# Eight shared PSUM banks divided into four and four, and VectorE's element-wise operations in the form with three operands

## The chip, the core and the metric

The kernel runs on one core of a Trainium2 chip, in one launch. The metric is the device time of the execution in microseconds (us), read on the chip. The engines are TensorE (PE; PEld is its loading of weights), VectorE (DVE), ScalarE (ACT) and GpSimd (POOL); SyncE (SP) issues most of the DMAs. PSUM, in which TensorE leaves its products, has eight banks of 512 float32 values on each of 128 partitions.

## What is computed

Two blocks of two layers each, on one sequence of 1024 tokens with 1024 channels, all in float32:

```python
def reference(x, ...):
    x = first_block(x, ...)
    return second_block(x, ...)

# first_block, twice:
h = rms_norm(x, norm_w[layer])
q, k, v, z_attn, q_h, f_h, i_h, g_h, gate_attn, gate_hgrn = split(h @ w_in[layer])
a = sliding_window_attention(rope(q), rope(k), v, sinks) * silu(z_attn)
b = rms_norm(hgrn2_recurrence(silu(q_h), k_of(f_h), i_h, logf)) * w * silu(g_h)
merged = sigmoid(gate_attn) * (a @ w_up_attn[layer]) + sigmoid(gate_hgrn) * (b @ w_up_hgrn[layer])
x = x + merged @ w_out[layer]
# and a last rms_norm

# second_block, layer 0:
u, v, z = split(rms_norm(x, g) @ w_in)
x = x + (gelu(u) * (W_s @ layer_norm(gelu(v)) + b) * silu(z)) @ w_out
# layer 1: k and v of the stream; each chunk of 64 tokens attends to itself and 8 chunks before
x = x + (chunk_attention(q, k, v, bias) * silu(z)) @ w_out
# and a last rms_norm
```

The sliding-window attention has 8 query heads and 2 key heads of 64 channels and a window of 128; the chunk attention has 16 heads of 64.

## The kernel before

Activations lie transposed (channels on partitions, 512 tokens to a tile) in tiles of 128x512 float32 from one heap of 61 (`hp`). For accuracy every operand of a large product is split in a rounded part and a rest, `hi` and `lo` (for weights `wh` and `wl`): `lo = x - hi` is an element-wise subtraction, and each product is three matmuls. Weights come from HBM through `raw` tiles (three buffers) and are split into eight `wh` and eight `wl` tiles.

The Python program is a list of units. A unit loads and splits its weights, two units ahead of its use, takes a PSUM tile with `mm()`, sets its matmuls (`unit`, L261 to L263, 512 columns or, in the last part, 256; `unit_tok`, L275 to L277, 256 columns; `unit_wide`, L289 to L291), and gives the result to a small function that evicts it. All other work is written as generators ("fibers"), which advance a step for every 24 matmuls or so (in the chunk attention 8). What they put in PSUM goes into tiles of `aux()`: means of squares over the channels (L383, L1027 and, for the first quarter and the second of the tokens, L1163), transposed keys (L573) and queries, scores of the sliding window (L634), levels of the recurrence (L703), a bias of the gMLP layer (L1234, L1239) and the chunk attention's scores (L1424), transposed probabilities (L1460) and output (L1470). `mm()` and `aux()` take their tiles from one ring of eight:

```python
    def mm(self):
        return self.ps.tile([P, H], F32, tag="bank", bufs=8, name=self.name("mm"))
    def aux(self):
        return self.ps.tile([P, H], F32, tag="bank", bufs=8, name=self.name("aux"))
```

So the tile that is ninth in the program waits until the first has been read, whichever of the two it is. Engines work on their own queues; the order of instructions on each queue is set ahead of the run by a list scheduler, which takes the program's order, the dependencies and its own estimates of time, and may set a later matmul ahead of an earlier one whose operand it expects later. It doesn't set an instruction ahead if that needs a buffer which is still in use.

Element-wise work is given to VectorE, GpSimd or ScalarE by a running account of booked time (`Engine.load`, `least`). All calls of an engine pass one helper, so that in the profile nearly all rows but TensorE's have its line, L76; tiles tell them apart. `khl` is a split key of one block of 128 tokens (two buffers), `ropea` and `ropeb` are parts of the rotation, `sP` the probabilities and `pT` their transposed form.

In the chunk attention the work goes by blocks of one pair of heads and 128 queries, 64 in all: two or four score tiles, a softmax, up to four tiles of transpositions, one output tile `po`, which ScalarE copies out. At the very end `out_last` (L1000) makes the output in quarters of 256 tokens: product, residual, sum of squares, mean (L1027), scaling, store.

Of the kernel before, what the change touches and what calls it, by code (L numbers as in the profile page):

```python
# [9 lines left out]
F32 = mybir.dt.float32  # L10
# [4 lines left out]
ALU = mybir.AluOpType  # L15
# [4 lines left out]
P = 128  # L20
H = 512
# [60 lines left out]
class Chip:  # L82
# [5 lines left out]
    def least(self, names, method, n):  # L88

        return min((getattr(self, k) for k in names), key=lambda e: e.load + e.price(method, n))  # L90

    def spend(self, ns):
        for e in (self.vector, self.scalar, self.gpsimd):
            e.load = max(0.0, e.load - ns)


class Net:
# [44 lines left out]
        return self.heap(F32R), self.heap(F32R)  # L142

    def mm(self):
        return self.ps.tile([P, H], F32, tag="bank", bufs=8, name=self.name("mm"))

    def aux(self):
        return self.ps.tile([P, H], F32, tag="bank", bufs=8, name=self.name("aux"))

    def half_banks(self):  # L150

# [47 lines left out]
    def tt(self, out, in0, in1, op):  # L199

        e = self.nc.least(("vector", "gpsimd"), "tensor_tensor", int(np.prod(out.shape[1:])))
        e.tensor_tensor(out=out, in0=in0, in1=in1, op=op)

    def split(self, src, hi, lo, hsrc=None):
        self.copy(hi, src)
# [191 lines left out]
    def square_sum(self, acc, x, k, scale=None):  # L397
        nc = self.nc
        if k == 0:
            acc = self.heap()  # L400
            sq = acc
        else:
            sq = self.heap()
        if scale is None:
            nc.scalar.activation(out=sq, in_=x, func=AF.Square)
        else:
            nc.scalar.activation(out=sq, in_=x, func=AF.Square, scale=scale)
        if k:
            nc.vector.tensor_add(acc, acc, sq)
        return acc  # L410

    @contextmanager
# [587 lines left out]
    def out_last(self, ws, wload, rhs, xsrc, gain):  # L1000

        nc = self.nc
        Q = 256
        xs = {}
        pair = lambda t, k, qs: t[2 * k : 2 * k + 2, 1, :, qs].rearrange("k p t -> p k t")

        def run(q, j):
            qs = slice(q * Q, (q + 1) * Q)
            if q == 0 and j < KD - AHEAD:
                wload(j + AHEAD)  # L1010
            if j % 2 == 0:
                xs[j // 2] = self.heap().rearrange("p (k t) -> p k t", k=2)
                nc.sync.dma_start(out=xs[j // 2], in_=pair(xsrc, j // 2, qs))
            ps = self.mm()[:, :Q]
            self.unit(ps, ws[j], [[None, tuple(t[:, qs] for t in r[1])] for r in rhs], 1)
            x = xs[j // 2][:, j % 2, :]
            nc.vector.tensor_add(x, ps, x)
            sq = self.heap()[:, :Q]
            nc.scalar.activation(out=sq, in_=x, func=AF.Square)
            if j == 0:  # L1020
                xs["acc"] = sq
            elif j < KD - 1:
                nc.vector.tensor_add(xs["acc"], xs["acc"], sq)
            else:
                po = self.aux()[:, :Q]
                for i, t in enumerate((xs["acc"], sq)):
                    nc.tensor.matmul(po, self.ones_f, t, start=(i == 0), stop=(i == 1))  # L1027
            nc.scalar.activation(out=x, in_=x, func=AF.Copy, scale=gain(j))
            if j == KD - 1:
                r = self.rstd_of(po, Q)  # L1030
                for k in range(KD // 2):
                    x = xs[k]
                    (nc.gpsimd if k == 1 else nc.vector).tensor_tensor(
                        out=x, in0=x, in1=r[:, None, :].to_broadcast([P, 2, Q]), op=ALU.mult
                    )
                    (nc.nc.scalar if k % 2 and q else nc.sync).dma_start(out=pair(self.out, k, qs), in_=x)
            self.tick(1.5 * len(rhs))

        for q in range(2):
            for j in range(KD):  # L1040
                self.units.append((None, lambda w, q=q, j=j: run(q, j)))
# [18 lines left out]
    def scaled_split(self, xs, ks, gain, rstd, res, half):  # L1060
        nc = self.nc
        for k in ks:
            t = xs[k]
            if gain is None:
                nc.vector.tensor_mul(t, t, rstd[half])
            else:
                nc.vector.scalar_tensor_tensor(
                    out=t, in0=t, scalar=gain(k), in1=rstd[half], op0=ALU.mult, op1=ALU.mult
                )
            res[k][half] = self.split_pair(t)  # L1070
        yield
# [67 lines left out]
    def load_first(self, res):  # L1139

        nc = self.nc
        Q = 256
        xs = [self.heaps(KD // 2) for _ in range(2)]
# [8 lines left out]
        def squares(q):  # L1152
            acc = None
            for x in xs[q]:
                sq = self.heap()
                nc.scalar.activation(out=sq, in_=x, func=AF.Square)
                if acc is None:
                    acc = sq
                else:
                    nc.vector.tensor_add(acc, acc, sq)  # L1160
            ps = self.aux()[:, :Q]
            for i in range(2):
                nc.tensor.matmul(ps, self.ones_f, acc[:, i * Q : (i + 1) * Q], start=(i == 0), stop=(i == 1))  # L1163
            return ps

        def scale(q, r):
            o = slice(q * Q, (q + 1) * Q)
            for k in range(KD):
                x = xs[q][k // 2][:, (k % 2) * Q : (k % 2) * Q + Q]
                nc.vector.scalar_tensor_tensor(  # L1170
                    out=x, in0=x, scalar=self.col("norm_w", k), in1=r, op0=ALU.mult, op1=ALU.mult
                )
                if q == 0:
                    res[k][0] = self.pair()
                hi, lo = res[k][0]
                nc.scalar.copy(out=hi[:, o], in_=x)
                e = nc.gpsimd if k % 2 else nc.vector
                e.tensor_tensor(out=lo[:, o], in0=x, in1=hi[:, o].bitcast(F32), op=ALU.subtract)

        r = self.rstd_of(squares(0), Q)  # L1180
        root = self.root
# [62 lines left out]
    def gmlp_half(self, h, half, y, ready):  # L1244
        nc, a = self.nc, self.a
# [42 lines left out]
        def mix(hd, z, u, wm, bias):  # L1288
            yield
            self.finish(st["ln"])  # L1290
            pm = self.aux()
            s = slice((hd % 4) * P, (hd % 4) * P + P)
            for t in range(4):
                nc.tensor.matmul(pm[:, t * P : (t + 1) * P], v[t][hd // 4][:, s], wm[:, s], start=True, stop=True)
            m = self.heap()
            nc.vector.scalar_tensor_tensor(
                out=m.rearrange("p (g t) -> p g t", g=4), in0=pm.rearrange("p (g t) -> p g t", g=4),
                scalar=self.col("a_ln_g", hd), in1=bias[:, None, s].to_broadcast([P, 4, P]),
                op0=ALU.mult, op1=ALU.add,
            )  # L1300
            yield
            nc.vector.tensor_mul(m, m, u)
            self.tt(m, m, z, ALU.mult)
            y[hd][half] = self.split_pair(m)

# [409 lines left out]
```

## Time and profile before

| | us |
|---|---|
| median of three runs (3022.23 to 3022.83) | 3022.28 |
| the profiled execution | 3024.32 |
| its span, from the first instruction to the last | 3022.5 |
| TensorE busy | 2927.0 |
| VectorE busy | 1678.1 |
| ScalarE busy | 1449.5 |
| GpSimd busy | 1091.5 |

Busy time counts the time in which an engine executes; the chain that ended last goes over TensorE for 89% of the span and over VectorE for 4%. The mean granted clock of TensorE over the span is 0.99 of its full speed (2.4 GHz); the profile has it in shares of that.

### The profile page before, as it was taken

What the parts mean: (1) busy time and instruction counts of PE and PEld (TensorE: products, weight loads), DVE (VectorE), ACT (ScalarE), POOL (GpSimd) and SP (SyncE); (2) the same over time, 40 slices, a digit from 0 to 9 for tenths busy, and PEclk for the clock granted to TensorE, in tenths of its full rate; (3) what the DMA queues carried; (4) which work ended last, traced back from release to release, by engine and by line L of the source; (5) the groups of instructions that cost most, each with busy time, mean ns of one, the idle gap of its engine ahead of it and who ended that gap; (6) DMA issues with size and microseconds to landing.
All of it is one profiled execution on the core that took longest, in us unless ns stands there. A gap on an engine that the chain in (4) does not pass through costs nothing.

```text
span 3022.5 us, 43638 instructions
## 1 busy us (share of the span) xinstructions
PE 2927.0 (97%) x16188; PEld 2432.3 (80%) x16188; DVE 1678.1 (56%) x3298; ACT 1449.5 (48%) x2927; POOL 1091.5 (36%) x1174
## 2 busy tenths in 40 slices
PE   6999999999999999999999999999999799999997
PEld 5887887888878888788888878888888688878777
DVE  6556745556556666665666533445344644454566
ACT  4665325642357434475334455334544545564552
POOL 4445333543435433444332233213332322232331
PEclk9999999999999999999999999999999899999999
DMA  3212242122522224212243222533234111111123
GB/s 113 84 63 93 89 147 82 66 70 91 182 70 71 73 84 151 99 70 70 74 151 132 101 92 97 166 103 129 95 116 159 56 38 60 38 59 44 64 98 112
DMA packets 101493, 283.47 MB, mean 94 GB/s; under 512 B 11288, under 2 KB 15512, under 8 KB 101280
## 3 DMA queue, kind: packets, MB, share of 16 engines
q1 hardware_dynamic: 100016, 279.51, 27.3%
q8 instruction: 128, 2.10, 0.3%
q10 hardware_dynamic: 1264, 1.17, 0.1%
q14 instruction: 85, 0.70, 0.1%
HBM read 259.66 MB, written 20.97 MB: 93 GB/s over the span
## 4 chain that ended last, share of the span: by engine, by line
PE 89%; DVE 4%; issue 2%; POOL 2%; DMA 1%; ACT 1%; SPq 0%; DVEq 0%; POOLq 0%; ACTq 0%
PE mm L261 20%; PE mm L262 20%; PE mm L263 20%; PE mm L289 3%; PE mm L290 3%; PE mm L291 3%; DVE hp L76 3%; PE aux L703 2%; PE aux L1470 2%; PE aux L1424 2%; PE mm L275 2%; PE aux L1460 2%; PE mm L276 1%; PE mm L277 1%; PE aux L634 1%
## 5 line engine op out<-in xcount | busy, mean ns | idle before, releaser
L261 PE MATMUL mm<-hp,wh 128*128 128x512 f32 (+1 forms) x2816 | 1118.8, 397 | 0.0
L262 PE MATMUL mm<-hp,wh 128*128 128x512 f32 (+1 forms) x2816 | 1093.2, 388 | 2.0 <-POOL hp L76 2.0
L263 PE MATMUL mm<-hp,wl 128*128 128x512 f32 (+1 forms) x2816 | 1093.7, 388 | 0.0
L76 POOL TENSOR_TENSOR wl<-raw,wh 128x512 fp32r<-128x512 f32 x369 | 491.3, 1334 | 800.7 <-ACT wh L76 690.7
L76 ACT CAST wh<-raw 128x512 fp32r<-128x512 f32 x584 | 360.4, 620 | 692.5 <-PE mm L262 467.1
L76 POOL TENSOR_TENSOR hp<-hp,hp 128x256 f32<-128x256 f32 (+3 forms) x347 | 380.5, 1102 | 680.1 <-DVE hp L76 240.3
L261 PEld LDWEIGHTS mm<-hp,wh 128*128 128x128 f32 x2816 | 530.7, 188 | 114.9 <-issue 11.2
L263 PEld LDWEIGHTS mm<-hp,wl 128*128 128x128 f32 x2816 | 530.0, 188 | 110.9 <-issue 0.2
L262 PEld LDWEIGHTS mm<-hp,wh 128*128 128x128 f32 x2816 | 531.1, 189 | 102.0 <-POOL hp L76 3.3
L76 DVE TENSOR_TENSOR wl<-raw,wh 128x512 fp32r<-128x512 f32 x447 | 358.8, 805 | 231.8 <-ACT wh L76 188.7
L76 DVE TENSOR_TENSOR hp<-hp,hp 128x512 f32<-128x512 f32 (+2 forms) x407 | 296.3, 737 | 154.9 <-ACT hp L76 109.3
L76 ACT ACT_TABLE_LOAD x244 | 313.1, 1283 | 22.9 <-PE mm L263 10.5
L76 DVE TENSOR_TENSOR hp<-mm,hp 128x512 f32<-128x512 f32 (+2 forms) x264 | 166.6, 637 | 161.1 <-ACT hp L76 79.3
L76 ACT ACTIVATE hp<-mm 128x512 f32<-128x512 f32 (+2 forms) x304 | 171.4, 574 | 170.0 <-PE mm L291 78.8
L76 DVE CAST wh<-raw 128x512 fp32r<-128x512 f32 x232 | 118.9, 513 | 186.9 <-PE mm L262 148.9
L76 ACT CAST hp<-hp 128x512 fp32r<-128x512 f32 (+1 forms) x206 | 116.0, 574 | 217.9 <-POOL hp L76 179.8
L76 POOL TENSOR_SCALAR sP<-sP,a2l 128x640 f32<-128x640 f32 (+4 forms) x128 | 89.0, 697 | 284.4 <-DVE a2l L76 176.7
L289 PE MATMUL mm<-wh,hp 128*128 128x512 f32 x480 | 188.1, 392 | 0.0
L290 PE MATMUL mm<-wl,hp 128*128 128x512 f32 x480 | 188.1, 392 | 0.0
L291 PE MATMUL mm<-wh,hp 128*128 128x512 f32 x480 | 187.8, 391 | 0.0
L76 ACT ACTIVATE sP<-sP,a2nm 128x640 f32<-128x640 f32 (+4 forms) x128 | 88.3, 691 | 101.1 <-DVE a2nm L76 101.0
L275 PE MATMUL mm<-wh,hp 128*128 128x256 f32 x448 | 133.7, 298 | 0.0
(186 smaller groups left out, 3406.0 us busy)
## 6 DMA issues: line engine op xcount, KB each, us to landing
raw<-in_w_ch_dram SPq DMA_DIRECT2D x128, 512.0 KB, 3.3
raw<-in_g_uz_dram SPq DMA_DIRECT2D x64, 512.0 KB, 3.3
hp<-xd SPq DMA_DIRECT2D x88, 256.0 KB, 4.2
raw<-in_w_up_dram SPq DMA_DIRECT2D x64, 256.0 KB, 2.7
raw<-in_w_o_dram SPq DMA_DIRECT2D x32, 512.0 KB, 3.3
raw<-in_g_v_dram SPq DMA_DIRECT2D x32, 512.0 KB, 4.0
raw<-in_g_o_dram SPq DMA_DIRECT2D x32, 512.0 KB, 3.8
raw<-in_w_wide_dram SPq DMA_DIRECT2D x28, 512.0 KB, 3.9
```

Source lines behind the costliest of these rows:

```text
L76: self.last = f(*args, **kw)
L261: nc.tensor.matmul(ps, wh[:, c : c + P], rh, start=(k == 0), stop=False)
L262: nc.tensor.matmul(ps, wh[:, c : c + P], rl, start=False, stop=False)
L263: nc.tensor.matmul(ps, wl[:, c : c + P], rh, start=False, stop=(k == nk - 1))
L275: nc.tensor.matmul(ps, lh[:, o : o + P], wh[:, c : c + n], start=(k == 0), stop=False)
L289: nc.tensor.matmul(ps, lh[:, s], wh, start=(k == 0), stop=False)
L290: nc.tensor.matmul(ps, lh[:, s], wl, start=False, stop=False)
L291: nc.tensor.matmul(ps, ll[:, s], wh, start=False, stop=(k == KD - 1))
L703: nc.tensor.matmul(ps[:, s], k[:, s], q[:, s], start=True, stop=True)
L1424: nc.tensor.matmul(ps[:, 0:w], lhs[r, o : o + P], rhs[r, k0 : k0 + w], start=(j == 0), stop=(j == 2))
L1460: nc.tensor.transpose(ps[:, j * P : (j + 1) * P], S[:, (i + j) * P : (i + j + 1) * P], self.ident)
L1470: nc.tensor.matmul(po[e * 64 : e * 64 + 64, 0:P], vv, pts[e][:, i * P : (i + 1) * P], start=(i == 0), stop=(i == nb - 1),)
```

## The change

The ring of eight banks becomes two of four, one for the units' products and one for everything else. And where VectorE combines two tensors in SBUF by a sum, a difference or a product, the instruction is `scalar_tensor_tensor`, `(in0 * 1.0) op in1`, in place of `tensor_tensor`, `in0 op in1`; operations that read PSUM keep their form, and GpSimd's too. The new helper is `Chip.ew`.

```diff
+    def ew(self, out, in0, in1, op):
+        self.vector.scalar_tensor_tensor(out=out, in0=in0, scalar=1.0, in1=in1, op0=ALU.mult, op1=op)
...
     def mm(self):
-        return self.ps.tile([P, H], F32, tag="bank", bufs=8, name=self.name("mm"))
+        return self.ps.tile([P, H], F32, tag="mm", bufs=4, name=self.name("mm"))
     def aux(self):
-        return self.ps.tile([P, H], F32, tag="bank", bufs=8, name=self.name("aux"))
+        return self.ps.tile([P, H], F32, tag="aux", bufs=4, name=self.name("aux"))
...
         e = self.nc.least(("vector", "gpsimd"), "tensor_tensor", int(np.prod(out.shape[1:])))
-        e.tensor_tensor(out=out, in0=in0, in1=in1, op=op)
+        if e is self.nc.vector:
+            self.nc.ew(out, in0, in1, op)
+        else:
+            e.tensor_tensor(out=out, in0=in0, in1=in1, op=op)
...
         if k:
-            nc.vector.tensor_add(acc, acc, sq)
+            nc.ew(acc, acc, sq, ALU.add)
...
-                e = nc.gpsimd if k % 2 else nc.vector
-                e.tensor_tensor(out=lo[:, o], in0=x, in1=hi[:, o].bitcast(F32), op=ALU.subtract)
+                sub = nc.gpsimd.tensor_tensor if k % 2 else nc.ew
+                sub(out=lo[:, o], in0=x, in1=hi[:, o].bitcast(F32), op=ALU.subtract)
```

The same replacement stands in the sums of squares of `out_last` and `load_first`, in `scaled_split` and in the gMLP layer's product with `u`. Lines behind the helper move by a few numbers: L1163 becomes L1170, L573 L580, L634 L641, L1424 L1431.

The order of instructions changes on all queues. Three places follow. In the first a name has the number of its allocation only, in the others the tile's own number as well.

The first is the start, on TensorE. Before, the mean of the second quarter (`aux_209`) stands second, ahead of every unit:

```order
L1163 MATMUL aux_132<-hp_121,ones_f 128x256 x2
L1163 MATMUL aux_209<-hp_198,ones_f 128x256 x2
L275 MATMUL mm_299<-wh_142,hp_159 128x256
L276 MATMUL mm_299<-wl_143,hp_159 128x256
L277 MATMUL mm_299<-wh_142,hp_160 128x256
L275 MATMUL mm_299<-wh_142,hp_164 128x256
```

Now all matmuls of the two units `mm_299` and `mm_332` (24 each, with the hi and lo parts of the first quarter) and one of `mm_359` stand ahead of it; these are the rows around it:

```order
L283 MATMUL mm_332<-wl_155,hp_189 128x256
L284 MATMUL mm_332<-wh_154,hp_190 128x256
L282 MATMUL mm_332<-wh_154,hp_194 128x256
L283 MATMUL mm_332<-wl_155,hp_194 128x256
L284 MATMUL mm_332<-wh_154,hp_195 128x256
L282 MATMUL mm_359<-wh_221,hp_159 128x256
L1170 MATMUL aux_209<-hp_198,ones_f 128x256 x2
L283 MATMUL mm_359<-wl_222,hp_159 128x256
L284 MATMUL mm_359<-wh_221,hp_160 128x256
L282 MATMUL mm_359<-wh_221,hp_164 128x256
```

So the mean of the second quarter has moved 49 rows back.

The second is the first block of the chunk attention, on TensorE: `aux4253` and `aux4254` are its first scores, of the queries `hp4243` and `hp4244`. `mm4242` is the product that gives the first keys, `mm4260` one of values. Before:

```order
L262 MATMUL mm4242_20524<-hp4152_20027,wh4208_20413 128x512
L263 MATMUL mm4242_20524<-hp4151_20026,wl4209_20414 128x512
L1424 MATMUL aux4253_20567<-hp4243_20549,hp4240_20520 128x256
L1424 MATMUL aux4254_20568<-hp4243_20549,hp4240_20520 128x256
L275 MATMUL mm4260_20597<-wh4211_20421,hp4105_19829 128x256
L1424 MATMUL aux4253_20567<-hp4244_20550,hp4240_20520 128x256
L1424 MATMUL aux4254_20568<-hp4244_20550,hp4240_20520 128x256
L1424 MATMUL aux4253_20567<-hp4243_20549,hp4241_20521 128x256
L1424 MATMUL aux4254_20568<-hp4243_20549,hp4241_20521 128x256
L276 MATMUL mm4260_20597<-wl4212_20422,hp4105_19829 128x256
L277 MATMUL mm4260_20597<-wh4211_20421,hp4106_19830 128x256
```

Now these rows stand around the first scores:

```order
L282 MATMUL mm4262_20624<-wh4218_20441,hp4151_20026 128x256
L283 MATMUL mm4262_20624<-wl4219_20442,hp4151_20026 128x256
L284 MATMUL mm4262_20624<-wh4218_20441,hp4152_20027 128x256
L282 MATMUL mm4273_20676<-wh4211_20421,hp4105_19829 128x256
L1431 MATMUL aux4253_20567<-hp4243_20549,hp4240_20520 128x256
L1431 MATMUL aux4254_20568<-hp4243_20549,hp4240_20520 128x256
L1431 MATMUL aux4253_20567<-hp4244_20550,hp4240_20520 128x256
L1431 MATMUL aux4254_20568<-hp4244_20550,hp4240_20520 128x256
L1431 MATMUL aux4253_20567<-hp4243_20549,hp4241_20521 128x256
L1431 MATMUL aux4254_20568<-hp4243_20549,hp4241_20521 128x256
```

All 24 matmuls of `mm4260`, all 24 of `mm4262` and one of `mm4273` have moved ahead of the scores.

The third is the beginning of the second half of the tokens in the first block's second layer, at 1228 us, on GpSimd. `hp2363` holds two blocks of keys, `khl2383` and `khl2399`, `khl2400` split ones; `hp2395` and `hp2396` are queries. Before:

```order
L76 TENSOR_TENSOR wl2340_11194<-raw2336_11187,wh2339_11193 128x512
L76 TENSOR_TENSOR hp2363_11263<-ropea2386_11402,ropeb2387_11403 128x2x16
L76 TENSOR_TENSOR ropea2401_11506<-hp2395_11468,cos_493 128x64
L76 TENSOR_TENSOR ropeb2402_11507<-hp2395_11468,sin_494 128x4x8 x2
L76 TENSOR_TENSOR hp2395_11468<-ropea2401_11506,ropeb2402_11507 128x4x16
L76 TENSOR_TENSOR ropea2412_11604<-hp2396_11470,cos_493 128x64
L76 TENSOR_TENSOR ropeb2413_11605<-hp2396_11470,sin_494 128x4x8 x2
L76 TENSOR_TENSOR hp2396_11470<-ropea2412_11604,ropeb2413_11605 128x4x16
L76 TENSOR_TENSOR hp2405_11536<-hp2395_11468,hp2405_11536 128x4x64
L76 TENSOR_TENSOR khl2399_11496<-hp2363_11263,khl2399_11496 128x128 x2
L76 TENSOR_TENSOR khl2400_11501<-hp2363_11263,khl2400_11501 128x128 x2
```

Now:

```order
L76 TENSOR_TENSOR khl2382_11386<-hp2363_11263,khl2382_11386 128x128 x2
L76 TENSOR_TENSOR khl2383_11391<-hp2363_11263,khl2383_11391 128x128 x2
L76 TENSOR_TENSOR wl2340_11194<-raw2336_11187,wh2339_11193 128x512
L76 TENSOR_TENSOR khl2399_11496<-hp2363_11263,khl2399_11496 128x128 x2
L76 TENSOR_TENSOR khl2400_11501<-hp2363_11263,khl2400_11501 128x128 x2
L76 TENSOR_TENSOR ropea2401_11506<-hp2395_11468,cos_493 128x64
L76 TENSOR_TENSOR ropeb2402_11507<-hp2395_11468,sin_494 128x4x8 x2
L76 TENSOR_TENSOR hp2395_11468<-ropea2401_11506,ropeb2402_11507 128x4x16
L76 TENSOR_TENSOR ropea2412_11604<-hp2396_11470,cos_493 128x64
L76 TENSOR_TENSOR ropeb2413_11605<-hp2396_11470,sin_494 128x4x8 x2
L76 TENSOR_TENSOR hp2396_11470<-ropea2412_11604,ropeb2413_11605 128x4x16
L76 TENSOR_TENSOR hp2405_11536<-hp2395_11468,hp2405_11536 128x4x64
```

The subtractions of `khl2399` and `khl2400` have moved ahead of the rotation of the queries; on ScalarE their casts have moved in the same way ahead of the eviction of the queries.

## Rows read from the trace of the kernel before

**Rows 1.** The page, busy time of each engine, its share and instructions.

```profile
PE 2927.0 (97%) x16188; PEld 2432.3 (80%) x16188; DVE 1678.1 (56%) x3298; ACT 1449.5 (48%) x2927; POOL 1091.5 (36%) x1174
```

**Rows 2.** TensorE in order of time, 7 to 45 us: start, length, instructions [idle before].

```profile
27.15 2.08 PE L1163 MATMUL aux<-hp,ones_f 128*128 128x256 f32 x4 [17.40 <-DVE hp L76]
```

**Rows 3.** TensorE in order of time, 2344 to 2371 us.

```profile
2343.70 0.39 PE L262 MATMUL mm<-hp,wh 128*128 128x512 f32 x1
...
2346.64 0.39 PE L263 MATMUL mm<-hp,wl 128*128 128x512 f32 x1
2363.40 0.58 PE L1424 MATMUL aux<-hp,hp 64*128 64x256 f32 x2 [16.37 <-ACT hp L76]
...
2367.63 0.28 PE L275 MATMUL mm<-wh,hp 128*128 128x256 f32 x1
...
2370.98 0.28 PE L276 MATMUL mm<-wl,hp 128*128 128x256 f32 x1
```

**Rows 4.** Waits of TensorE: line, releaser: total us, times, longest.

```profile
PE aux L573 <- POOL khl L76: 7.6, 5, 3.0
PE aux L634 <- ACT hp L76: 4.4, 11, 0.9
...
PE aux L1239 <- ACT hp L76: 3.1, 4, 1.1
```

**Rows 5.** Stretches: busy us of PE, PEld, DVE, ACT, POOL (instructions), clock, DMA share, GB/s.

```profile
1207.00:1210.40 3.40, 3.40 (x19) 3.40 (x18) 1.28 (x1) 2.35 (x4) 3.09 (x11) 0.51 0.00 0
...
1230.90:1237.80 6.90, 6.51 (x20) 5.16 (x21) 2.65 (x7) 2.17 (x9) 1.58 (x4) 0.51 0.10 38
1691.70:1695.10 3.40, 3.40 (x10) 2.68 (x9) 2.94 (x8) 1.90 (x3) 0.00 (x0) 0.50 0.57 200
...
2372.00:2875.00 503.00, 502.08 (x3586) 411.69 (x3586) 244.09 (x860) 265.21 (x686) 141.40 (x186) 1.00 0.15 53
...
2985.40:2988.80 3.40, 3.40 (x16) 3.22 (x15) 2.71 (x4) 1.19 (x3) 0.00 (x0) 0.50 0.80 298
```

**Rows 6.** TensorE in order of time, 1201 to 1234 us.

```profile
1205.79 0.50 PE L383 MATMUL aux<-hp,ones_d 128*128 128x512 f32 x1 [3.48 <-DVE hp L76]
...
1227.98 0.28 PE L573 MATMUL aux<-identr,khl 128*128 128x128 f32 x1 [2.20 <-ACT khl L76]
1231.29 0.91 PE L573 MATMUL aux<-identr,khl 128*128 128x128 f32 x4 [3.03 <-POOL khl L76]
```

**Rows 7.** TensorE in order of time, 2978 to 2990 us.

```profile
2984.81 0.70 PE L1027 MATMUL aux<-hp,ones_f 128*128 128x256 f32 x2 [2.58 <-DVE hp L76]
```

**Rows 8.** VectorE's groups by form: busy us, mean ns, idle us before them.

```profile
L76 DVE TENSOR_TENSOR wl<-raw,wh 128x512 fp32r<-128x512 f32 x447 | 358.8, 805 | 231.8 <-ACT wh L76 188.7 <-PE aux L383 14.8 <-PE aux L784 12.8
...
L76 DVE TENSOR_TENSOR hp<-hp,hp 128x512 f32<-128x512 f32 x139 | 119.1, 872 | 39.6 <-ACT hp L76 27.6 <-DMA hp<-xd 8.8
...
L76 DVE SCALAR_TENSOR_TENSOR hp<-hp,hp 128x512 f32<-128x512 f32 x52 | 45.9, 883 | 0.5
```

**Rows 9.** Waits of TensorE from 59 to 72 us.

```profile
PE aux L573 <- POOL khl L76: 4.6, 4, 2.1
```

**Rows 10.** All engines in order of time, 1225 to 1232 us.

```profile
1224.96 0.76 POOL L76 TENSOR_TENSOR ropea<-hp,cos 128x64 f32<-128x64 f32 x1 [7.25 <-ACT hp L76]
...
1227.50 1.00 ACT L76 CAST khl<-hp 128x128 fp32r<-128x128 f32 x4
...
1230.79 1.28 POOL L76 TENSOR_TENSOR khl<-hp,khl 128x128 fp32r<-128x128 f32 x3
```

**Rows 11.** VectorE in order of time, 2993 us to the end.

```profile
2999.85 0.76 DVE L76 TENSOR_TENSOR hp<-mm,hp 128x256 f32<-128x256 f32 x2 [2.93 <-DMA hp<-xd]
```

**Rows 12.** All engines in order of time, 2495 to 2497 us.

```profile
2495.75 1.32 PE L1424 MATMUL aux<-hp,hp 64*128 64x256 f32 x12
2495.90 0.27 ACT L76 COPY hp<-aux 128x128 f32<-128x128 f32 x1 [0.91 <-PE aux L1470]
```

More of the change, by code (lines that the diff above doesn't have):

```diff
@@ L1022, in run @@
             elif j < KD - 1:
-                nc.vector.tensor_add(xs["acc"], xs["acc"], sq)
+                nc.ew(xs["acc"], xs["acc"], sq, ALU.add)
             else:
@@ L1064, in scaled_split @@
             if gain is None:
-                nc.vector.tensor_mul(t, t, rstd[half])
+                nc.ew(t, t, rstd[half], ALU.mult)
             else:
@@ L1159, in squares @@
                 else:
-                    nc.vector.tensor_add(acc, acc, sq)
+                    nc.ew(acc, acc, sq, ALU.add)
             ps = self.aux()[:, :Q]
@@ L1301, in mix @@
             yield
-            nc.vector.tensor_mul(m, m, u)
+            nc.ew(m, m, u, ALU.mult)
             self.tt(m, m, z, ALU.mult)
```

## The prediction

> **What bounds the kernel now.** I read the page's busy line first. TensorE (PE) is busy 2927.0 us [rows 1] of a span of 3022.5 us; VectorE (DVE), the next, 1678.1 us. So the time is PE's matmuls plus 95.5 us in which PE stands, and only two things can move it: those 95.5 us, and the speed at which PE runs. From the page alone, making VectorE's operations dearer or cheaper should hardly show, unless one of them is what PE waits for.
>
> Next the list of PE's waits. The long ones are few: 17.40 us at L1163 (start) [rows 2], 16.37 us at L1424 (start of the chunk attention) [rows 3], 7.6 us in all at L573, 4.4 at L634, 3.1 at L1239 [rows 4]. All of these lines write an `aux` tile and wait for an operand: the sums of squares, a rotated key, a transposed query. I followed each to the tile named as releaser, and none is a bank of PSUM that has yet to be read. So with eight shared banks no wait is for a bank.
>
> Third, the stretches around these waits, for their granted clock. After a wait it is often half (1.2 GHz, 0.50 or 0.51 in the profile) for a while: 3.40 us from 1207.0, 6.90 us from 1230.9, 3.40 us from 1691.7 and from 2985.4 [rows 5]; what goes before each is an idle stretch of PE (3.48 us; 2.20 and 3.03 us; one of the four waits of L1239; 2.58 us [rows 4, 6, 7]). In 3.40 us at half clock PE does what takes 1.7 us at 2.4 GHz. So a wait that is filled with matmuls may give back 1.7 us more than its own length.
>
> **The change, part by part.**
>
> **1. The form with three operands.** By the order of the changed kernel 745 operations of VectorE take it; nothing else about them changes, and the planner that shares work among the engines books the same price, so no operation changes its engine. The trace has both forms, on the same tiles: the three-operand form 128x512 costs 883 ns in the mean (52 of them), the plain one 872 ns (139) [rows 8]. Working in from both sides: 11 ns more on 745 operations is 8 us of VectorE's busy time, and if the 447 weight subtractions (805 ns) came to 883 ns it would be 35 us; if all came to 805 ns or below, nothing or a gain. VectorE has 1344 us of idle time (3022.5 less 1678.1) to cover it; uncovered is only what stands in a chain that PE waits for, by the order some ten operations each in the norms at the start, at two layers' ends and at the end: 40 operations at 11 ns, 0.4 us. I take 0 (-3 to +3).
>
> Here a page of the skill bears on the row. The Trainium skill, "SBUF — State Buffer", section "SBUF: two separate sides", says that a VectorE operation with two SBUF inputs and a GpSimd operation that reads SBUF lock each other out of a shared port pair for a whole instruction. Both forms have two SBUF inputs, so by this rule the change frees GpSimd of nothing, and the trace agrees as far as it goes: the three-operand form's mean of 883 ns is no shorter than the plain one's 872 ns [rows 8]. Were the new form to hold no lock, GpSimd would be the gainer, and what PE waits for GpSimd is the 7.6 us at L573 [rows 4]: the forecast would come out up to 8 us lower.
>
> **2. Two PSUM pools: what moves.** A new unit of matmuls (`mm`) no longer needs the bank that a transposition or a score (`aux`) was to leave, so the scheduler is free to set it earlier. By the order, 494 of PE's 14,680 matmuls move, most of them `mm` matmuls that now stand ahead of an `aux` matmul which waits. The price of one with 256 columns is 0.12 us: 29 starts from 2367.63 to 2370.98, 3.35/28; with 512 columns 0.226 us: 14 starts from 2343.70 to 2346.64, 2.94/13 [rows 3]. Place by place:
>
> - **Start.** 49 matmuls (all of two units) now stand ahead of the second mean (L1163), inside its wait of 17.40 us [rows 2]; their inputs come by 22.85 us at the latest, by the ends of the operations that write them. That makes PE reach the keys (L573) some 6 us or more earlier, but these wait for GpSimd's rotations, 4.6 us in all, 2.1 the longest [rows 9], and those come when they come. So what is kept is what can be done in that second wait: 24 matmuls of a unit that stood behind it, 2.9 us at full and up to 5.8 us at half clock, and what GpSimd gains by two weight subtractions that moved ahead of the rotations' chain. I take 5 (0 to 8).
> - **1205 us.** 21 matmuls move ahead of L383, 21 x 0.12 = 2.5 of the 3.48 us [rows 6]; the half clock behind it should go with the wait: 1.7 [rows 5]. 4 (2.5 to 4.2).
> - **1228 us.** Two key tiles (`khl2399`, `khl2400`) were cast and subtracted after the rotation of the queries; they now go first. PE waited 2.20 + 3.03 us for them [rows 6], while GpSimd rotated queries from 1224.96 to 1230.79 [rows 10]. The casts still wait until PE has read the two earlier key tiles, whose buffers they take; a microsecond after 1224.96 is my estimate for that. Then they take 1.00 us on ScalarE, and their subtractions 1.28 us for three of four on GpSimd, so 1.7 [rows 10], so PE starts at about 1228.3 in place of 1231.29: 3, and about 2 of the 3.4 us that the half clock takes of 6.90 [rows 5]. 5 (0 to 8.3).
> - **L634.** In each of the waits of 0.9 us four 512-column matmuls move ahead (4 x 0.226 = 0.9), in those of 0.2 us one. All 4.4 us [rows 4].
> - **L1239.** The same in four places: 3.1 [rows 4] and 1.7 for the half clock at 1691.7 [rows 5]: 4.8 (3.1 to 4.8).
> - **2363 us.** 48 matmuls of two units, ready before the wait, go into its 16.37 us [rows 3]: 48 x 0.12 = 5.7. Some 10 us of wait remain, and the half clock after it.
> - **End.** 24 matmuls move ahead of L1027: 2.58 of waiting [rows 7] and 1.7 of half clock [rows 5], 4.3. But VectorE then stands 2.93 us for the residual stream's DMA until 2999.85 [rows 11], and PE's last units need the four `mm` banks that VectorE empties. I take 2.5 (0 to 4.3).
>
> Sum: 5 + 4 + 5 + 4.4 + 4.8 + 5.7 + 2.5 = 31.4; all upper ends 39.7, all lower ends 15.7.
>
> **3. Two PSUM pools: what it costs.** Four banks must now hold all transpositions, scores and means. I went through all `aux` tiles with the times of this trace and asked whether the tile four places back had been read when the next was begun. It had, but for ten places, which together lack 5.2 us, none more than 0.8; five lie at the end of the chunk attention, four at L634, where two matmuls have been put in between. Some 29 more in the chunk attention have under 0.5 us: in one of them the block's output leaves its bank by a copy from 2495.90 to 2496.17, while the next block's scores, of which the fourth needs this bank, have been running since 2495.75 [rows 12]. The change has nothing there to hide a stall: PE is busy 502.08 of 503.00 us [rows 5]. Bounds: 0 (the order within a block gives way) to 5.2 + 29 x 0.27 (a whole copy each) = 13. I take 2.5, nearer to the places that the trace shows as short.
>
> Net: 31.4 - 2.5 = 29. The profiled execution took 3024.3 us, 1.8 more than its span; less 29 it is 2995. The runs before lie 2.0 below it, at 3022.3: **2993 us**.
>
> **The rivals.** About 0.2% (6 us) is what a measurement of this kernel can tell from no change.
>
> *The waits come back elsewhere* (0.17). Three of the gains end at a chain that PE doesn't set: GpSimd's rotations at the start, the keys at 1228, the DMA at the end. If these three give nothing and the rest half, it is 0.5 x (4 + 4.4 + 4.8 + 5.7) = 9.5, less 2.5: 7, so 3015 us. For it speaks that every one of these waits has its releaser on another engine; against it that 1205, L634, L1239 and 2363 have matmuls ready to go in. Between it and the forecast lies 3004.
>
> *Four banks starve the attention* (0.08). The chunk attention goes through 64 blocks with up to five `aux` tiles each for scores and output and more for transpositions. If each block lost 0.5 us, 32 us would go and the kernel would end at 3022.3 - 31.4 + 32 = 3023; from 0.6 us for a block (38 us) it is slower by over 0.2%: 3029. The point at which it decides is thus twice the 0.27 us of the copy in [rows 12], in every block. For it: L1470's copies and L1424's scores follow each other without a gap. Against: fewer than 40 of those tiles are near the edge. The Trainium skill, "Perfetto Trace Analysis", section "Matmul Optimizations", asks to use all eight PSUM banks for the sake of parallelism. All eight stay in use here, but each kind of tile can reach only four; no wait in [rows 4] is for a bank, so the trace so far doesn't bear the rule out.
>
> *The new form is slower where it counts* (0.04). 35 us more on VectorE, with a tenth of it uncovered, takes 3.5 us: 2997, inside the forecast's range.
>
> *Nothing happens* (0.03): the scheduler's order is not what the chip's time hangs on. 3022; against it, each wait filled is idle time in the trace.
>
> **How the numbers follow.** Forecast 0.68, with 2982 (all upper ends) to 3006 (15.7 in gains and nothing lost) as its own range. The range for 8 in 10 takes in most of the first rival: 2981 to 3014. Faster by over 0.2% (below 3016): 0.68 + 0.04 + about two thirds of 0.17, 0.84. Slower: half of the second rival and a share of mishaps, 0.06. Within: the rest, 0.10.
>
> **What would show it.** PE's list of waits should have L634 and L1239 gone or below 1 us, the longest at L573 at about 2 us, and the long wait before the first scores near 10 to 11 us; PE's busy time should fall by some 5 us for the half-clock stretches that are gone at 1207, 1691 and 2985. New rows "PE aux L1431" or "PE aux L1467" (the lines of scores and transpositions after the change) with many small waits on ScalarE or VectorE between 2350 and 2870 us would be the banks' price; over 10 us in them makes the prediction wrong. The three-operand form should show means of 800 to 900 ns on weights; if GpSimd's busy time falls or rises by more than 30 us, part 1 is wrong.

## The result

The changed kernel takes 2993.7 us in the median of four runs (2991.4 to 2996.5), against 3022.6 for the kernel before: a ratio of 0.9903, with a 95% interval of 0.9886 to 0.9920. Forecast were 2993 us, in a range of 2981 to 3014. The profiled execution of the changed kernel took 2991.4 us, with a span of 2989.6 us; it is the fastest of the four, while the profiled execution of before lay 1.8 us above its median, so that the span is 32.9 us shorter, some 3.5 us more than the ratio says.

The busy times stand in the page's first section:

```profile
PE 2925.9 (98%) x16188; PEld 2427.6 (81%) x16188; DVE 1681.3 (56%) x3298; ACT 1447.3 (48%) x2927; POOL 1094.8 (37%) x1174
```

Against [rows 1] no engine's busy time moves by more than 3.3 us. So 32.9 us went, and 31.8 of them were idle time of TensorE, which is 63.7 us now.

The list of TensorE's waits after the change (line, releaser: total us, times, longest), whose lines are those of before plus 7:

```profile
PE mm L282 <- DVE hp L76: 9.5, 1, 9.5
PE aux L1170 <- DVE hp L76: 8.7, 2, 7.7
PE aux L390 <- DVE hp L76: 8.2, 6, 4.7
PE mm L282 <- ACT hp L76: 7.2, 1, 7.2
PE mm L269 <- POOL hp L76: 4.7, 4, 1.9
PE aux L580 <- POOL khl L76: 3.8, 7, 2.0
PE aux L580 <- ACT khl L76: 3.1, 1, 3.1
...
PE aux L1034 <- DVE hp L76: 0.9, 1, 0.9
```

The waits of L634 and L1239 [rows 4], now L641 and L1246, are gone from it altogether. TensorE in order of time at the places of [rows 2, 3, 6], and one block of the chunk attention (start, length, instructions [idle before]):

```profile
16.93 0.58 PE L282 MATMUL mm<-wh,hp 128*128 128x256 f32 x1 [7.16 <-ACT hp L76]
...
27.24 1.13 PE L1170 MATMUL aux<-hp,ones_f 128*128 128x256 f32 x4 [1.03 <-DVE hp L76]
...
1198.52 0.47 PE L390 MATMUL aux<-hp,ones_d 128*128 128x512 f32 x1 [1.36 <-DVE hp L76]
...
1216.84 0.28 PE L580 MATMUL aux<-identr,khl 128*128 128x128 f32 x1 [0.50 <-POOL khl L76]
...
2338.65 0.58 PE L282 MATMUL mm<-wh,hp 128*128 128x256 f32 x1 [9.47 <-DVE hp L76]
...
2466.23 1.42 PE L1431 MATMUL aux<-hp,hp 64*128 64x256 f32 x12
```

TensorE's wait of 17.40 us before the second mean has become 7.16 before the first units and 1.03 before the mean; that of 3.48 us is 1.36; that of 16.37 us is 9.47, and what waits is no longer the first score but the third tile of values. The last row is dealt with further down.

The granted clock tells the other part of the gain. These stretches lie where those of [rows 5] lay, 7 to 35 us earlier:

```profile
1199.60:1203.00 3.40, 3.40 (x28) 3.31 (x27) 1.25 (x1) 3.25 (x5) 2.96 (x10) 1.00 0.00 0
1215.50:1222.40 6.90, 6.30 (x30) 5.09 (x30) 6.35 (x10) 5.35 (x23) 6.74 (x13) 1.00 0.40 151
1670.00:1673.40 3.40, 3.40 (x18) 2.58 (x17) 3.37 (x14) 2.14 (x3) 1.26 (x1) 1.00 0.34 112
2343.10:2846.00 502.90, 502.14 (x3567) 412.27 (x3567) 242.20 (x852) 263.14 (x678) 140.54 (x186) 1.00 0.15 53
2951.00:2954.40 3.40, 3.40 (x31) 3.40 (x30) 3.29 (x6) 0.00 (x0) 0.00 (x0) 1.00 0.00 0
```

All four that ran at half clock, 0.50 or 0.51, run at full clock, 1.00, in this execution; not all do in another one (below). In 3.40 us at the end TensorE now starts 31 matmuls where it started 16.

The new form, in VectorE's groups by form (busy us, mean ns):

```profile
L76 DVE SCALAR_TENSOR_TENSOR wl<-raw,wh 128x512 fp32r<-128x512 f32 x447 | 360.1, 808 | 223.9 <-ACT wh L76 182.6 <-PE aux L390 14.8 <-PE aux L791 12.8
L76 DVE SCALAR_TENSOR_TENSOR hp<-hp,hp 128x512 f32<-128x512 f32 x185 | 155.3, 850 | 39.9 <-ACT hp L76 27.2 <-DMA hp<-xd 8.9
```

The weight subtractions take 808 ns in place of 805 [rows 8]; the 185 operations of the second row are the old 52 and 133 converted ones, at 850 ns where the two groups had 883 and 872.

**Where the time came from.** The two kernels have the same matmuls, so each unit of one trace can be matched by its tile to that of the other, and the time of its last matmul compared. The lead of the changed kernel, in us, by the time in the trace of before; the last column is the lead in a second profiled execution of the same kernel, the run "the change, again" of the next section:

| up to | lead | gained on the way | lead, again |
|---|---|---|---|
| 72 us, the start | 3.5 | 3.5 | 2.3 |
| 1202 us, three norms, three sets of L634 and of L573 | 7.7 | 4.2 | 5.2 |
| 1211 us, L383 | 11.6 | 3.9 | 6.7 |
| 1245 us, L573 | 18.2 | 7.0, less 0.3 lost ahead of it | 10.1 |
| 1603 us, the last L634 | 19.0 | 1.3, less 0.5 | 10.9 |
| 1849 us, L1239 in four places | 23.6 | 4.6 | 14.5 |
| 2376 us, first scores | 29.9 | 6.3 | 21.3 |
| 2901 us, chunk attention | 27.3 | -2.6 | 18.6 |
| 2925 us | 28.8 | 1.5 | 20.1 |
| 2990 us, L1027 | 34.1 | 5.3 | 25.0 |
| end of the span | 32.9 | -1.2 | 23.8 |

The second execution was the slowest of its four, 3000.5 us, on a chip on which the kernel before takes 5 us longer too; but places differ, not only the total. At 1205 us it gains 0.4 us where the first gains 3.6. The mean there hangs on VectorE's last sum of the residual stream, which waits for a DMA: 0.90 us before the change, 1.08 us in the first execution, 2.60 us in the second. Before, after, and again, with TensorE's wait for that mean in the last row:

```profile
1202.65 0.69 DVE L76 TENSOR_TENSOR hp<-mm,hp 128x512 f32<-128x512 f32 x1 [0.90 <-DMA hp<-xd]
1195.29 0.69 DVE L76 TENSOR_TENSOR hp<-mm,hp 128x512 f32<-128x512 f32 x1 [1.08 <-DMA hp<-xd]
1199.57 0.69 DVE L76 TENSOR_TENSOR hp<-mm,hp 128x512 f32<-128x512 f32 x1 [2.60 <-DMA hp<-xd]
1202.80 0.74 PE L390 MATMUL aux<-hp,ones_d 128*128 128x512 f32 x1 [3.14 <-DVE hp L76]
```

And the half clock stayed in two of the four places, those at 1205 and 1228 us of before's time:

```profile
1202.80:1206.20 3.40, 3.40 (x14) 3.21 (x15) 0.58 (x1) 2.33 (x7) 3.01 (x9) 0.50 0.00 0
1223.30:1226.70 3.40, 3.24 (x8) 2.64 (x9) 1.70 (x3) 0.57 (x2) 3.24 (x10) 0.50 0.23 82
```

### The profile page after: what moved, and what is told of

Same layout as the page of the kernel before. It is cut to its first block, busy times and chain, and to the rows that moved or that the text cites. A ratio compares the mean times of both kernels' runs of the same rounds, so it can differ in the third digit from the quotient of the medians.

```text
span 2989.6 us, 43665 instructions
## 1 busy us (share of the span) xinstructions
PE 2925.9 (98%) x16188; PEld 2427.6 (81%) x16188; DVE 1681.3 (56%) x3298; ACT 1447.3 (48%) x2927; POOL 1094.8 (37%) x1174
## 4 chain that ended last, share of the span: by engine, by line
PE 92%; DVE 4%; issue 1%; POOL 1%; DMA 1%; ACT 1%; SPq 0%; DVEq 0%; POOLq 0%; ACTq 0%
PE mm L268 21%; PE mm L269 21%; PE mm L270 21%; PE mm L298 4%; PE mm L297 4%; PE mm L296 3%; DVE hp L76 3%; PE aux L1431 2%; PE aux L710 2%; PE aux L1477 2%; PE aux L1467 2%; PE mm L282 1%; PE mm L283 1%; PE mm L284 1%; PE aux L641 1%
## 5 line engine op out<-in xcount | busy, mean ns | idle before, releaser
L76 DVE SCALAR_TENSOR_TENSOR wl<-raw,wh 128x512 fp32r<-128x512 f32 x447 | 360.1, 808 | 223.9 <-ACT wh L76 182.6
L76 DVE SCALAR_TENSOR_TENSOR hp<-hp,hp 128x512 fp32r<-128x512 f32 (+3 forms) x349 | 272.9, 789 | 115.8 <-ACT hp L76 101.7
L282 PE MATMUL mm<-wh,hp 128*128 128x256 f32 x448 | 133.2, 297 | 16.6 <-DVE hp L76 9.5
```

The source lines that it names most:

```text
L76: self.last = f(*args, **kw)
L282: nc.tensor.matmul(ps, lh[:, o : o + P], wh[:, c : c + n], start=(k == 0), stop=False)
```

## The experiments

Each is given with the ratio to the kernel before, run beside it on the same chip, and its 95% interval. They ran in three sets on two chips, in which the kernel before took 3025.2, 3027.6 and 3028.3 us, so that ratios are compared and not times. The first set has pools alone, form alone, the order of one ring and three and five; the second the change again, four and three, the output tiles and the normalization held back; the third the other two. The ratio of the change itself was 0.9903 with the result and 0.9896 here, that of pools alone, with the same order, 0.9905: differences below 0.002 or so, 6 us, can't be read from the ratios alone. "The attention" is the time from the end of the unit `mm4273` to that of `mm5635`, the 525 us in which the blocks run; the kernel before takes 525.6, the changed one 528.2.

| kernel | ratio | interval | attention, us |
|---|---|---|---|
| the change, again | 0.9896 | 0.9883 to 0.9910 | 528.2 |
| pools alone | 0.9905 | 0.9891 to 0.9918 | 528.3 |
| form alone | 1.0002 | 0.9993 to 1.0010 | 525.6 |
| pools, order of one ring | 1.0022 | 1.0014 to 1.0031 | 528.8 |
| four and three | 0.9988 | 0.9979 to 0.9997 | 551.1 |
| three and five | 0.9921 | 0.9907 to 0.9934 | 527.4 |
| output tiles in the products' pool | 0.9892 | 0.9879 to 0.9906 | 525.9 |
| scores first | 0.9913 | 0.9899 to 0.9928 | |
| normalization held back | 0.9873 | 0.9858 to 0.9888 | |
| held back, and output tiles moved | 0.9874 | 0.9858 to 0.9891 | |

The change again, beside the second set of experiments:

> The whole change once more, beside the others on the same chip: 0.990 of the kernel before.

It came out at 0.9896.

**The two halves apart.** First the pools with the plain form:

```diff
-            self.nc.ew(out, in0, in1, op)
+            e.tensor_tensor(out=out, in0=in0, in1=in1, op=op)
```

and so in the other places.

> The two PSUM pools of four alone; VectorE keeps the plain form everywhere. The order of every engine is that of the whole change. My theory (the form is worth nothing, the pools give all): 2994 us, within 3 of the whole change, with the same waits of TensorE. Rival (the form frees or slows something that counts): over 5 us away from the whole change, and VectorE's or GpSimd's busy time 30 us away from it.

Then the form with one ring:

```diff
-        return self.ps.tile([P, H], F32, tag="mm", bufs=4, name=self.name("mm"))
+        return self.ps.tile([P, H], F32, tag="bank", bufs=8, name=self.name("mm"))
-        return self.ps.tile([P, H], F32, tag="aux", bufs=4, name=self.name("aux"))
+        return self.ps.tile([P, H], F32, tag="bank", bufs=8, name=self.name("aux"))
```

> The form with three operands alone; one ring of eight PSUM banks as before. The order of every engine is that of the kernel before. My theory: 3022 us, within 3 of the kernel before. Rival (the form matters): over 5 us away from it, to either side.

0.9905 and 1.0002: the pools give all of it, the form nothing that can be measured. The form alone keeps the long waits of before, L641's 4.4 and L1246's 3.1 us among them.

**The banks without the order.** Each tile of PSUM is begun behind the tile that precedes it in the program, by an edge that orders the queue and waits for nothing:

```diff
+            for prev in reversed(self.tiles[: self.tiles.index(name)]):
+                if prev in self.first:
+                    self.tc.add_manual_dep(
+                        ins.ins, self.first[prev].name,
+                        mybir.DependencyInfo(mybir.DependencyClass.NoSync, mybir.DependencyReason.DATA), reason="ring",
+                    )
+                    break
```

> The whole change, but each tile of PSUM is begun only after the tile that precedes it in the program, whichever pool it is of, as one ring had it: so the banks are four and four and TensorE's order is that of the kernel before (14,664 of 14,682 matmuls in the same place). My theory (the gain is the order, and the banks themselves only cost): 3022 + 2 to 3 = 3025 us, with the old waits at the second mean, the first scores, the sliding window's scores and the bias. Rival (the gain comes from banks that are free earlier at run time, whatever the order): about 2994 us.

1.0022, 6.7 us above the kernel before: the rival falls. Its waits (all matmuls have the line of a helper, L105, transpositions L108):

```profile
PE aux L105 <- DVE hp L76: 40.6, 13, 17.4
PE aux L105 <- ACT hp L76: 24.9, 18, 16.6
PE aux L108 <- POOL khl L76: 7.8, 5, 3.0
```

17.4, 16.6 and 7.8 us answer to the waits of [rows 2, 3, 4]. With the same eight banks divided in the same way, the whole gain is gone with the order. And the price of the banks stands bare: 0.5 to 0.65 us at each of the four places of L634 where in the change two matmuls have been put in between, 2.4 in all, and 3.2 us in the attention. These 5.6 us answer to the 5.2 that the prediction had counted in the trace of before; the rest to 6.7 lies within the interval.

**The price of a bank.** One of the four banks that are not the products' is left unused:

```diff
-        return self.ps.tile([P, H], F32, tag="aux", bufs=4, name=self.name("aux"))
+        return self.ps.tile([P, H], F32, tag="aux", bufs=3, name=self.name("aux"))
```

> Four banks for the units' products, three for the rest, one bank unused. With the times of the first experiment's kernel, three banks would be short in some 70 places by about 60 us together, a good third of it in the chunk attention; the scheduler's order can give way in some of them. My theory (banks cost where a tile's last reader ends after the next tile is due): 20 to 60 us more than the whole change, 3014 to 3054, and the attention 15 us or more longer. Rival (the scheduler gives way and the number of banks hardly counts): within 5 us of the whole change.

0.9988, 29.5 us above the change beside it by the medians and 28 by the ratios, and the attention 22.9 us longer. The rival falls. How such a stall is read: not in the list of waits, which has in these 530 us two waits at the scores, of 0.9 and 0.2 us, but in the length of a group. The twelve matmuls of a block's scores, the same block as in the last row of the changed kernel above:

```profile
2478.47 2.07 PE L1431 MATMUL aux<-hp,hp 64*128 64x256 f32 x12
```

1.32 us before [rows 12], 1.42 with four banks, 2.07 with three. TensorE counts as busy through all of it: 531.14 of the 533.00 us from 2352 us.

**Three and five.** The fourth bank goes over to the other side:

```diff
-        return self.ps.tile([P, H], F32, tag="mm", bufs=4, name=self.name("mm"))
+        return self.ps.tile([P, H], F32, tag="mm", bufs=3, name=self.name("mm"))
-        return self.ps.tile([P, H], F32, tag="aux", bufs=4, name=self.name("aux"))
+        return self.ps.tile([P, H], F32, tag="aux", bufs=5, name=self.name("aux"))
```

> Three banks for the units' products and five for the rest. With the times of the changed kernel the fifth bank takes away all the short places of the chunk attention, where 2.6 us were lost; three banks for the products are short in 12 places by 30 us together, unless the scheduler's order gives way there. My theory (four banks for the rest cost 2.6 us in the attention): the attention from the first scores to its last block becomes 2 to 3 us shorter than with four and four; the whole lies between 2991 (products never wait) and 3020 us. Rival (the attention's loss is something else than banks): the attention keeps its length.

The attention is 0.8 us shorter, not 2 to 3. Unit by unit, though, the lead over the kernel before stands at 18.7 us from 2376 to 2637 us of its time and at 17.1 from 2708 to 2885, where the change loses 0.1 us at two of every eight blocks and 0.5 to 0.8 at two of the last; in between lies one step of 1.6 us. Of the two longest waits of this stretch the change has the first as well, so the step is the second:

```profile
PE mm L269 <- POOL hp L76: 1.8, 2, 0.9
PE aux L1467 <- ACT pT L76: 1.4, 1, 1.4
```

So the stalls of the banks are gone, as the theory has it, and a single wait of TensorE for a transposed tile (`pT`, copied by ScalarE) hides most of it in the sum. The whole is 5 us slower than pools alone in the same set and 8 us slower than the change by the ratios, at the edge of what they can tell: three banks for the products leave a wait of 13.5 us at the values in place of 9.5.

**Output tiles in the products' pool.**

```diff
-            po = self.aux()
+            po = self.mm()
```

> The whole change, with the output tile of each block of the chunk attention taken from the products' four banks in place of the other four. My theory (the short places of the attention are the scores that wait for this tile's copy): the attention loses its 2.6 us against the kernel before, the whole is 1 to 3 us below the change. Rival (a product then waits for a block's output to be begun, as in one ring): the attention becomes longer, the whole 3 us or more above the change.

The attention takes 525.9 us: 2.3 of the 2.6 us are back, so the output tile is what made it short of banks. The block's scores take 1.32 us again:

```profile
2468.50 1.32 PE L1431 MATMUL aux<-hp,hp 64*128 64x256 f32 x12
```

In the whole, 0.9892 against 0.9896 can't be told apart: behind the attention the lead falls by 1.9 us, at a wait of 1.9 us for a transposition (L1467 for ScalarE's `pT`) that the change hasn't. Why that wait comes up in some of these kernels is open; the kernel before has one of 1.2 us there.

**One place undone.** The values' matmuls are held behind the first of the scores:

```diff
-                self.unit_tok(ps[:, 0:256], x, w, t, 256)
+                with self.tc.issue_after(st["first"].ins):
+                    self.unit_tok(ps[:, 0:256], x, w, t, 256)
```

> The whole change with one place undone: the values' matmuls, of which 48 had moved ahead of the chunk attention's first scores, are held behind the first of these again. All else keeps its order but for single instructions. My theory (a filled wait gives back the price of what fills it): the long wait at the first scores is 16.4 us again and the whole 5 to 7 us above the change, 0.9915 of the kernel before. Rival (the wait only moves; the units' gain is taken back by the second half's queries): within 2 us of the change.

0.9913. The wait is back at the scores, with 14.1 us, not 16.4. The ratio alone doesn't decide: it is 5.1 us above the change of another set (0.9896) and 2.4 above pools alone (0.9905), and the intervals overlap. Unit by unit, from 2300 to 2356 us, this run loses 6.2 us to the first trace of the change, 6.7 to the second and 5.1 to that of pools alone, and so the rival falls. The term of the prediction for this place was 5.7 us, the trace of the change gave 6.3.

**What is left of that wait.** In the changed kernel the 49th matmul waits, for the bank of the first queries. VectorE in order of time:

```profile
2325.55 10.89 DVE L76 SCALAR_TENSOR_TENSOR hp<-hp,hp 128x512 f32<-128x512 f32 x9
2337.90 0.69 DVE L76 SCALAR_TENSOR_TENSOR hp<-mm,hp 128x512 fp32r<-128x512 f32 x1 [1.47 <-ACT hp L76]
```

The queries' product is complete at 2318; its last reader on VectorE (`hp<-mm,hp`) starts at 2337.90, behind a normalization of 10.89 us, and TensorE starts 0.75 us later. On ScalarE too, the queries' eviction lies behind the eight casts of that normalization. It belongs to the second half of the tokens, which is needed later. So it was held back:

```diff
             if at_once and half:
+                for _ in range(8):
+                    yield
                 yield from self.scaled_split(xs, range(KD), gain, rstd, res, half)
```

> The whole change, with the normalization of the second half of the tokens, ahead of the chunk attention, held back by eight steps of its fiber, so that ScalarE and VectorE empty the first queries and keys before they go on to that normalization and not behind it. My theory (the 9.5 us that are left of the long wait are ScalarE's and VectorE's queues, in which the queries' bank is emptied last): that wait falls below 3 us, and the whole is 4 to 8 us below the change, since the second half's queries then wait a little for their input. Rival (the wait moves whole to the second half's queries): within 2 us of the change.

0.9873, 7 us below the change in the same set by the ratios and 4.3 by the medians; the intervals just overlap. Unit by unit, from 2300 to 2400 us, it gains 8.0 us on the change of that set, 8.5 on the first trace of the change and 9.6 on pools alone. VectorE now reads the queries' product between the steps that lead to the normalization, 7 us earlier, in an execution that was 6.9 us behind the other until then:

```profile
2330.76 0.68 DVE L76 SCALAR_TENSOR_TENSOR hp<-mm,hp 128x512 fp32r<-128x512 f32 x1
```

and the wait is gone from TensorE:

```profile
2331.87 0.39 PE L1433 MATMUL aux<-hp,hp 64*128 64x256 f32 x2 [0.53 <-ACT hp L76]
```

Both edits at once, this one and the output tiles:

> Both edits that helped together: the normalization of the second half held back, and the attention's output tiles in the products' banks. My theory (they act at different places, so they add up): 2 us below the run with the first alone, 0.9865 of the kernel before. Rival (the attention is shorter, but the last blocks and the last layer then wait for their own chain): no less than with the first alone, 0.987 to 0.988.

0.9874 against 0.9873: no gain shows, but the 2 us expected are less than what ratios of two sets can tell, so neither theory nor rival is shown. In the traces the lead over the kernel before falls by 0.9 us from 2400 to 2901 us of its time, against 3.0 us with the first edit alone; and three waits for transpositions (L1469 for `pT`), 3.0 us in all, stand where the first alone has 2.0. Holding the normalization back is the smallest version that beats both kernels, by 1.27% over the kernel before.

## Why the prediction was right

**What bounds the kernel** held: 31.8 of the 32.9 us are idle time of TensorE. The half clock is the smaller and less certain part.

**Part 1, the form** held: 808 and 850 ns, 1.0002 alone, GpSimd's busy time up by 3.3 us. The two bounds of -3 and +3 us were enough. 744 operations took the form, not 745 (VectorE's plain ones went from 1509 to 765).

**Part 2, the terms.** Measured in the first trace against forecast: the start 3.5 (5), 1205 us 3.9 (4), 1228 us 7.0 (5), L634 and with it L573 in two places some 4.7 (4.4 for L634), L1239 4.6 (4.8), 2363 us 6.3 (5.7), the end 4.1 (2.5). They sum to 34.1 against 31.4. In the second execution the same places sum to some 26, with 2.3 at the start, 0.4 at 1205, 4.6 at 1228, 3.6 at L1239, 6.8 at 2363 and 3.7 at the end. The forecast lies between the two, and so does the ratio of the medians, 0.9903, which is 29 us, what the prediction had net. That the first trace met the term of 1205 us so closely is luck: the prediction put the DMA of the residual stream into its sum at the end alone, and at 1205 us it sets the mean too, with 2.60 us in the second execution, so that the wait stayed at 3.14 us and the half clock with it. The start was rated too high since its second wait did not fill: from 45 to 75 us TensorE waits 3.1 us for ScalarE's split keys and 3.1 for GpSimd's at L580, once the matmuls ahead of them are done, where before it waited 4.6 [rows 9]; and it runs at half clock for 10.2 us there in place of 6.8. At 1228 TensorE waited for the moved keys hardly at all (0.50 us at 1216.84), because the casts began sooner than the microsecond estimated, at 1214.27, 0.55 us after the transpositions of the earlier keys, and the subtractions overlapped them. (Laid end to end, the prediction's own figures give 1228.7 and not 1228.3.) The half clock, which the estimate had left in part, went in the first trace and stayed in part in the second. The end came out near its upper bound: the DMA at 2999.85 [rows 11] did not hold it, since that wait, still 2.86 us, came 29.7 us earlier too. Two more gains were not in the sum, at 324 us (1.7, below) and around 2910 us (1.5, where a wait of 1.2 us for a transposition is gone), and a wait of 1.0 us for GpSimd at 387 us came in.

**Part 3, the banks** held: 2.6 us against 2.5, a choice between 0 and 13, so that the closeness is partly luck. Where the order is kept, all 5.6 come due, so the count of short places in the trace of before was a price and not a bound.

**One reason was wrong in its wording.** The prediction had it that a unit "no longer needs the bank that a transposition or a score (`aux`) was to leave". But no lack of a bank had held the units back. At the start, only two tiles precede the first unit in a ring of eight. In the order of before all 1298 tiles of PSUM are begun strictly in the program's order, without one exception; after the change there are 30 places where a later tile is begun first. So what one ring imposes on the scheduler is the order in which its tiles are begun, whether banks are free or not, and the second pool lifts this. The experiment with the pools and the old order shows on the chip that the gain hangs on this order. The forecast was not hurt, since it took its moves from the order itself.

**Three signs were wrong.** TensorE's busy time was to fall by some 5 us; it fell by 1.1, and in the second execution it is 2930.5 us, 3.5 more than before. The half-clock stretches that went did shorten it. Against them stand a longer one near the start (58.5 to 68.7 us), one behind the long wait, from 2331.7 to 2345.4 us, with 34 matmuls where that of before had 18, and the stalls of the banks, which count as busy; what each is worth in the sum was not worked out. The 48 matmuls that fill the long wait itself ran at full clock, 0.12 us apart. The stalls were to show as small waits at L1431; that list has 0.2 us. They show in the length of the groups. And the longest wait at L573 was to be about 2 us; it is 3.1, for ScalarE's split keys. The wait at the first scores, forecast at 10 to 11 us, was 9.47, but at another instruction, and for a bank of the products' four: a place where four are too few.

## What to carry to other kernels

With this scheduler, one pool for two kinds of tiles ties the order in which both are begun; where one kind waits for a slow chain and the other is ready, two pools let the scheduler fill the wait, and the price of the smaller pools can be counted ahead from the trace: for each tile, its first write less the end of the last read of the tile that will have had its bank. A wait that is filled is worth its filling, and sometimes the half clock that would have followed it: at two places here it went in one execution and stayed in another of the same kernel. So a term that is read from one trace wants a second trace. And when a wait shortens but stays, look for what now holds it: here it was an eviction that stood in two queues behind work that nobody needed yet.

## What was not expected of the hardware

The same two waits, some 0.8 and 0.7 us before two means, were followed by a half clock in some traces and not in others. Before, at 324.01 and 325.21 us (0.80 and 0.71 us of waiting), this stretch came behind them:

```profile
326.40:329.80 3.40, 3.40 (x10) 2.63 (x9) 1.89 (x1) 2.00 (x4) 1.28 (x1) 0.50 0.58 175
```

After, with the same waits at 319.67 and 320.87:

```profile
320.80:330.00 9.20, 9.13 (x40) 7.60 (x41) 7.65 (x11) 4.99 (x6) 1.29 (x1) 1.00 0.32 95
```

That is 1.7 us which no edit at this place accounts for. All twelve traces have these two waits, of 0.80 to 0.82 and of 0.71 us. Eight have the half clock behind them, among them pools alone, with the order of the change; four have not: the change, the change again, four and three, three and five. Those four, and no others, have the wait of 1.0 us for GpSimd at 387 us, which gives part of the 1.7 back. Waits of equal length don't decide the clock by themselves; what does was not tried.
